# Split weights at a chosen distance modulo 256 bytes, and squares written over dead tiles

## The chip, the cores and the metric

The kernel runs on one core of one Trainium2 chip. The metric is the device time of one execution in microseconds, from runs of the same program; one further execution was profiled, and all rows below come from it.

## What is computed

Two layers over 256 frames of width 2048, each an RMS norm, one wide input projection, two groups of mixers and an output projection that is added to the residual; a last RMS norm ends it. Cut to its frame:

```python
def layer_ab(x, ...):
    h = rms_norm(x, norm_g)
    proj = jnp.einsum('btd,de->bte', h, w_in)
    q, k, v, o_pre, z_a, i_pre, f_pre, z_b, xbc, dt_raw = split_cols(proj, SPLIT_AB)
    y_a = mlstm_branch(...)
    y_b = mamba2_branch(...)
    return x + jnp.einsum('bte,ed->btd', jnp.concatenate([y_a, y_b], -1), w_out)

def layer_cd(x, ...):
    h = rms_norm(x, norm_g)
    proj = jnp.einsum('btd,de->bte', h, w_in)
    q_c, ckv, z_c, iq, ik, iw, qkv, z_d, b_pre, a_pre = split_cols(proj, SPLIT_CD)
    y_c = dsa_branch(...)     # top-k attention; keys and values from ckv through w_uk, w_uv
    y_d = gdn_branch(...)     # gated delta rule; q and k are divided by their norms
    return x + jnp.einsum('bte,ed->btd', jnp.concatenate([y_c, y_d], -1), w_out)

return rms_norm(layer_cd(layer_ab(x)))
```

All of it is in float32, and the weights (390 MB) are read once.

## The kernel before

The projections make up most of the work. Weights come in pieces of 1 MB, `load_w`: a DMA fills `wr` (three buffers), ScalarE casts it to `wh` in the faster matmul type (line 191), and VectorE takes the difference `wl` (line 192). `wh` and `wl` have two buffers each, so a cast waits until TensorE is done with the piece before the last. Activations are split in the same way: `hT` (the normed input, 16 blocks of 128 rows), `cT` (the normed latent of the attention, 4 blocks) and the units `ua`, `ub`, `uc` (mixer outputs, 8 blocks each) hold 256 columns of the high part and 256 of the low part per block. A product takes three matmuls, high by high, high by low, low by high. All of them are issued through the helper at line 75; a transpose goes through line 79.

There are two forms. `proj_tok` yields tokens by features in `pt`: the activation is loaded into the array (128 columns) and 512 columns of the weight move through it. `proj_feat` yields features by tokens in `pf`: 128 columns of the weight are loaded, and 256 columns of the activation move. In the names of the trace the moving operand stands first behind the arrow (`pt<-wh,hT`, `pf<-hT,wh`). While one matmul runs, the operand of the next is loaded (PEld in the profile).

`out_proj` is `proj_tok` on a unit. `hT` feeds both forms in both layers, `cT` both forms in the attention. The mixers are generators on the list `steps`; `tick()` runs a piece of the first one between matmuls of the projections, so TensorE's order is interleaved by hand. The list `bg` holds the triangular solve of the delta rule, a long chain on VectorE; each `load_w` runs a piece of it through `pump()`, and a loop of 12 gate projections (`zk`, each `proj_tok` on `hT`) goes on meanwhile. `load_w`'s cast and difference have high priority in the scheduler, which otherwise orders instructions by what they wait for.

In the built program `hT` starts 192 bytes past a multiple of 256 in each partition, the units 160, `cT` 32, and all buffers of `wh` and `wl` 160. The slices that the matmuls read start at multiples of 512 bytes from there. `ones` is a tile of its own beside `tri`, whose right half is also all ones. `gjunk` is a scratch tile for squares whose sums alone are wanted, in the delta rule's query norms (`ssq`, from the transposes in the PSUM tile `qt`) and its output norms (`sso`); `vg` there holds the values.

Of the kernel before, what the change touches and what calls it, by code (L numbers as in the profile page):

```python
# [8 lines left out]
F32 = mybir.dt.float32  # L9
F32R = mybir.dt.float32r  # L10
I32 = mybir.dt.int32
AF = mybir.ActivationFunctionType
# [15 lines left out]
GONE = -3.4e38  # L28

KG, WR, WS = 4, 3, 2  # L30

STEPS = 1150

# [29 lines left out]
def trunk(ctx, tc, x, rel_bias, ab_norm, ab_w_in, ab_ml_b_i, ab_ml_b_f, ab_ml_norm, ab_ssm_conv_w,  # L63
# [4 lines left out]
    V, A, G = nc.vector, nc.scalar, nc.gpsimd  # L68
# [20 lines left out]
    cp = ctx.enter_context(tc.tile_pool(name="cp", bufs=1))  # L89
    wp = ctx.enter_context(tc.tile_pool(name="wp", bufs=3))  # L90
# [10 lines left out]
    tri = cp.tile([128, 256], F32, name="tri")  # L101
    V.memset(tri, 1.0)
    G.affine_select(tri[:, 0:128], tri[:, 0:128], pattern=[[1, 128]], compare_op=OP.is_ge, fill=0.0, base=0, channel_multiplier=-1)
    ones = cp.tile([128, 128], F32, name="ones")
    V.memset(ones, 1.0)

    def mx(name):
        return ps.tile([128, 512], F32, name=name, tag="mx")
# [67 lines left out]
        while steps:  # L176
            tick()

    def load_w(src, r0, nk, pieces, n):

        pump()
        shaped = lambda w: w.rearrange("p k n -> p (k n)").rearrange("p (k n) -> p k n", n=n)
        wr = shaped(wp.tile([128, KG, 512], F32, name="wr", tag="wr", bufs=WR))
        if sum(m for _, m, _ in pieces) < n:
            G.memset(wr[:, 0:nk, 0:n], 0.0)
        for c0, m, at in pieces:
            nc.sync.dma_start(wr[:, 0:nk, at:at + m], src[r0:r0 + nk * 128, c0:c0 + m].rearrange("(k p) n -> p k n", p=128))
        wh = shaped(wp.tile([128, KG, 512], F32R, name="wh", tag="wh", bufs=WS))
        wl = shaped(wp.tile([128, KG, 512], F32R, name="wl", tag="wl", bufs=WS))
        with tc.high_priority():  # L190
            A.copy(wh[:, 0:nk, 0:n], wr[:, 0:nk, 0:n])  # L191
            V.tensor_tensor(wl[:, 0:nk, 0:n], wr[:, 0:nk, 0:n], wh[:, 0:nk, 0:n].bitcast(F32), op=OP.subtract)  # L192
        return wh, wl

    def proj_tok(src, r0, X, c0, n=512, apart=False):

        pts = [ps.tile([128, 512], F32, name=f"pt{t}", tag="pt") for t in range(2)]
        nk = len(X)

        def part(w, k, t):  # L200
            (wh, wl), (xt, i) = w, X[k]
            hi, lo = xt[:, i, t * 128:t * 128 + 128], xt[:, i, 256 + t * 128:384 + t * 128]
            PE.matmul(pts[t][:, :n], hi, wh[:, k % KG, :n], start=k == 0, stop=False)
            PE.matmul(pts[t][:, :n], hi, wl[:, k % KG, :n], start=False, stop=False)
            PE.matmul(pts[t][:, :n], lo, wh[:, k % KG, :n], start=False, stop=k == nk - 1)

        if apart:

            w = [load_w(src, r0 + g * 128, KG, [(c0, n, 0)], n) for g in range(0, nk, KG)]
            for t in range(2):  # L210
                for k in range(nk):
                    part(w[k // KG], k, t)
                    tick()
            return pts
        for g in range(0, nk, KG):
            w = load_w(src, r0 + g * 128, KG, [(c0, n, 0)], n)
            if g + KG == nk:
                order = [(k, t) for t in range(2) for k in range(KG)]
            else:
                order = [(k, t) for k in range(KG) for t in range(2)]  # L220
            for i, (k, t) in enumerate(order):
                part(w, g + k, t)
                if i % 2:
                    tick()
        return pts

    def proj_feat(src, r0, X, pieces, groups=None):

        n = max(p[2] + p[1] for p in pieces)
        n = (n + 127) // 128 * 128  # L230
        nb = n // 128
        pts = [ps.tile([128, 512], F32, name=f"pf{b}", tag="pt") for b in range((nb + 1) // 2)]
        nk = len(X)
        kg = KG * 512 // n
        for g, m in groups or [(g, min(kg, nk - g)) for g in range(0, nk, kg)]:
            wh, wl = load_w(src, r0 + g * 128, m, pieces, n)
            last = g + m == nk
            order = [(k, b) for b in range(nb) for k in range(m)] if last else [(k, b) for k in range(m) for b in range(nb)]
            for at, (k, b) in enumerate(order):
                xt, i = X[g + k]  # L240
                bs = slice(b * 128, b * 128 + 128)
                pt = pts[b // 2][:, b % 2 * 256:b % 2 * 256 + 256]
                PE.matmul(pt, wh[:, k, bs], xt[:, i, 0:256], start=g + k == 0 and b % 2 == 0, stop=False)
                PE.matmul(pt, wh[:, k, bs], xt[:, i, 256:512], start=False, stop=False)
                PE.matmul(pt, wl[:, k, bs], xt[:, i, 0:256], start=False, stop=last and k == m - 1 and (b % 2 == 1 or b == nb - 1))
                if at % nb == nb - 1:
                    tick()
        return pts
# [145 lines left out]
    with ExitStack() as st:  # L394
        mp = st.enter_context(tc.tile_pool(name="mp", bufs=1))
        np1 = ExitStack()
        X, rb = normed(hT, gab, np1.enter_context(tc.tile_pool(name="np1", bufs=1)))
# [49 lines left out]
        pt = mx("RTp")  # L447
# [27 lines left out]
        for i in range(8):  # L475
            k = 1 << i
# [10 lines left out]
        pt = mx("R2Tp")  # L487
# [112 lines left out]
        with tc.tile_pool(name="lp", bufs=1) as lp:  # L600
# [71 lines left out]
            pt = mx("rbp")  # L672
# [10 lines left out]
            for h in range(4):  # L683
# [7 lines left out]
                v = lp.tile([128, 2, 512], F32, name="v", tag="v", bufs=2)  # L691
# [32 lines left out]
    with ExitStack() as st:  # L724
# [3 lines left out]
        X, rb = normed(hT, gcol[:, G_CD:G_CD + 16], kq)  # L728
# [181 lines left out]
        pt = mx("rkp")  # L910
# [197 lines left out]
        with tc.tile_pool(name="gp", bufs=1) as gp:  # L1108
# [13 lines left out]
            for i in range(4):  # L1122
                pts = proj_feat(cd_w_in, 0, X, [(CQKV + i * 512, 512, 0)])
                qc = gp.tile([128, 4, 256], F32, name="qc", tag="qc", bufs=QB)
                ssq = gp.tile([128, 2, 4], F32, name="ssq", tag="ssq", bufs=2)
                junk = gp.tile([128, 128], F32, name="gjunk", tag="gjunk")
                for b in range(2):
                    conv_gate(pts[b], gconv, i * 4 + b * 2, 64, None, qc[:, b * 2:b * 2 + 2].rearrange("p b t -> p (b t)"))
                rq = gp.tile([128, 8], F32, name="rq", tag="rq", bufs=2)
# [2 lines left out]
                def norms(qc, ssq, rq, rq2):  # L1132
                    yield from lag(LQ)
                    for j in range(4):
                        pt = mx("qt")
                        for t in range(2):
                            transpose(pt[:, t * 128:t * 128 + 128], qc[:, j, t * 128:t * 128 + 128])
                        for t in range(2):
                            A.activation(junk, pt[:, t * 128:t * 128 + 128], AF.Square, scale=0.5, accum_out=ssq[:, t, j:j + 1])
                        yield  # L1140

                    rsqrt(rq, ssq.rearrange("p t j -> p (t j)"), 1.0)
                    V.tensor_scalar(rq, rq, scalar1=0.5 * 128 ** -0.5, scalar2=None, op0=OP.mult)
                    V.tensor_tensor(rq2, rq, rq, op=OP.mult)

                steps.append(norms(qc, ssq, rq, rq2))
                for s in range(2):
# [47 lines left out]
                    o = gp.tile([128, 2, 512], F32, name="og_", tag="og_")  # L1195
                    z = gp.tile([128, 2, 512], F32, name="zg", tag="zg")

                    def delta(s, h0, qc, kT, k0, QD, Wt, vf, o, z, rq, rq2):
# [54 lines left out]
                        sso = gp.tile([128, 8], F32, name="sso", tag="sso", bufs=2)  # L1253
                        for c in range(2):
                            for h in range(4):
                                A.activation(junk, o[:, c, hsl[h]], AF.Square, accum_out=sso[:, c * 4 + h:c * 4 + h + 1])

                        dup = lambda r: r.rearrange("p (c j) -> p c j", c=2)[:, :, s * 2:s * 2 + 2].unsqueeze(3).to_broadcast([128, 2, 2, 2])
                        v4 = lambda r: r.rearrange("p (c j r) -> p c j r", c=2, j=2)
# [87 lines left out]
```

## Time and profile before

| | |
|---|---|
| median of 3 runs | 2158.25 us (2156.83 to 2161.36) |
| profiled execution | 2157.74 us, span 2156.0 us |
| granted clock, mean over the span | 0.992 |
| HBM | 389.87 MB read, 193 GB/s over the span |

The span runs from the first to the last instruction of the profile, and the execution's own time has 1.74 us around it. The granted clock is a share of 2.4 GHz. A matmul's printed duration covers its way through the array; consecutive matmuls overlap, so the time that each takes from the stream is the interval between two starts.

### The profile page before, as it was taken

To read this page: it belongs to the slowest core of one execution; us is meant where nothing else is said; L and a number is where in the kernel's file an instruction comes from. 1 tells how busy PE (TensorE), PEld (TensorE's weight loads), DVE (VectorE), ACT (ScalarE), POOL (GpSimd) and SP (SyncE) were. 2 spreads that over 40 slices of the span, in tenths; PEclk is the share of its full clock that TensorE was granted. 3 is DMA by queue.
4 is the path that set the end of the run, shared out by engine and by line. 5 is a ranking of instruction groups with operands and counts; after the bars stand their busy time and mean duration, and the time that the engine had idled before them with its cause. 6 is when DMAs were issued, how large, how long until landed. Compare 5 with 4: busy or idle time off the path is not lost.

```text
span 2156.0 us, 31526 instructions
## 1 busy us (share of the span) xinstructions
PE 2107.7 (98%) x12878; PEld 1861.2 (86%) x12878; DVE 1467.5 (68%) x2096; ACT 993.7 (46%) x1311; POOL 149.6 (7%) x168
## 2 busy tenths in 40 slices
PE   7999999999999999899999999999999999999997
PEld 6989997888889788898878888899898988989986
DVE  7888764555455456578979998555666666766765
ACT  5455443334433444355643333455444444444543
POOL 4000020000000000300100002000000000000001
PEclk9999999999999999999999999999999999999999
DMA  6565456555555555576886666755565555565543
GB/s 184 190 212 176 157 179 215 195 176 176 176 184 187 176 187 185 139 237 221 296 229 202 224 204 207 265 181 181 176 233 180 190 172 189 188 195 182 171 160 124
DMA packets 242342, 415.16 MB, mean 193 GB/s; under 512 B 45093, under 2 KB 69206, under 8 KB 240342
## 3 DMA queue, kind: packets, MB, share of 16 engines
q1 hardware_dynamic: 237254, 389.84, 55.4%
q0 software_dynamic: 4944, 23.31, 3.3%
q8 instruction: 101, 1.65, 0.3%
q14 instruction: 43, 0.35, 0.0%
HBM read 389.87 MB, written 26.38 MB: 193 GB/s over the span
## 4 chain that ended last, share of the span: by engine, by line
PE 85%; DVE 6%; ACT 3%; issue 1%; DMA 1%; ACTq 0%; SPq 0%
PE pt L75 49%; PE pf L75 27%; DVE wl L192 3%; ACT wh L191 2%; PE turn L79 1%; PE py L75 1%; PE pu L75 1%; PE si L75 1%; ACT Dt L862 1%; PE po L75 0%; PE lgt L75 0%; PE num L75 0%; PE pog L75 0%; DMA Dt<-gd 0%; PE vt L79 0%
## 5 line engine op out<-in xcount | busy, mean ns | idle before, releaser
L192 DVE TENSOR_TENSOR wl<-wr,wh 128x2048 fp32r<-128x2048 f32 (+1 forms) x337 | 777.1, 2306 | 482.6 <-ACT wh L191 479.1
L191 ACT CAST wh<-wr 128x2048 fp32r<-128x2048 f32 (+1 forms) x337 | 639.7, 1899 | 774.3 <-PE pt L75 455.4
L75 PE MATMUL pf<-hT,wh 128*128 128x256 f32 x4192 | 768.7, 285 | 0.3 <-POOL hT L296 0.2
L75 PEld LDWEIGHTS pf<-hT,wh 128*128 128x128 f32 x4192 | 650.2, 190 | 9.6 <-issue 5.7
L75 PE MATMUL pf<-hT,wl 128*128 128x256 f32 x2096 | 591.6, 283 | 14.6 <-DVE wl L192 14.6
L75 PE MATMUL pt<-wh,hT 128*128 128x512 f32 x1856 | 593.9, 398 | 0.0
L75 PEld LDWEIGHTS pt<-wh,hT 128*128 128x128 f32 x1856 | 349.2, 188 | 84.4 <-issue 1.9
L75 PEld LDWEIGHTS pf<-hT,wl 128*128 128x128 f32 x2096 | 398.2, 190 | 16.3 <-DVE wl L192 15.4
L75 PE MATMUL pt<-wl,hT 128*128 128x512 f32 x928 | 368.1, 397 | 1.3 <-DVE wl L192 1.3
L75 PE MATMUL pt<-wh,uc 128*128 128x512 f32 x768 | 250.4, 397 | 0.0
L75 PEld LDWEIGHTS pt<-wl,hT 128*128 128x128 f32 x928 | 174.7, 188 | 44.2 <-DVE wl L192 1.9
L75 PEld LDWEIGHTS pt<-wh,uc 128*128 128x128 f32 x768 | 143.9, 188 | 29.0 <-issue 0.5
L75 PE MATMUL pt<-wl,uc 128*128 128x512 f32 x384 | 151.2, 394 | 0.0
L381 DVE SCALAR_TENSOR_TENSOR cy<-pf,gconv,cy 128x255 f32<-128x255 f32 (+2 forms) x192 | 88.4, 477 | 5.3 <-ACT cy L377 3.1
L75 PEld LDWEIGHTS pt<-wl,uc 128*128 128x128 f32 x384 | 72.4, 188 | 13.6 <-DVE wl L192 0.4
L75 PE MATMUL pt<-wh,ua 128*128 128x512 f32 x256 | 80.0, 392 | 0.0
L75 PE MATMUL pt<-wh,ub 128*128 128x512 f32 x256 | 79.1, 389 | 0.0
L350 DVE TENSOR_TENSOR xr<-pt,xr 128x512 f32<-128x512 f32 x80 | 54.9, 686 | 25.5 <-PE pt L75 25.4
L75 PEld LDWEIGHTS pt<-wh,ub 128*128 128x128 f32 x256 | 48.1, 188 | 10.0
L1174 POOL TENSOR_TENSOR QD<-QD,qm 128x256 f32<-128x256 f32 x32 | 22.5, 739 | 491.7 <-DVE nrv L141 257.7
L75 PEld LDWEIGHTS pt<-wh,ua 128*128 128x128 f32 x256 | 47.9, 188 | 9.6
L296 POOL TENSOR_TENSOR hT<-xg,hT 128x512 fp32r<-128x512 f32 x24 | 40.8, 1711 | 201.7 <-issue 123.3
(457 smaller groups left out, 1868.8 us busy)
## 6 DMA issues: line engine op xcount, KB each, us to landing
wr<-in_cd_w_in_dram SPq DMA_DIRECT2D x140, 1024.0 KB, 5.1
wr<-in_ab_w_in_dram SPq DMA_DIRECT2D x87, 1024.0 KB, 5.2
wr<-in_cd_w_out_dram SPq DMA_DIRECT2D x48, 1024.0 KB, 5.1
wr<-in_ab_w_out_dram SPq DMA_DIRECT2D x32, 1024.0 KB, 5.1
wr<-in_ab_w_in_dram SPq DMA_DIRECT2D x33, 512.0 KB, 4.3
zd<-zk SPq DMA_DIRECT2D x12, 512.0 KB, 6.2
Dt<-gd SPq DMA_DIRECT2D x4, 1024.0 KB, 8.4
Dd<-Dt POOLq DMA_DIRECT2D x4, 1024.0 KB, 6.2
```

The lines of the kernel that those rows point to most:

```text
L75: return held(nc.tensor.matmul(*args, **kw))
L79: return held(nc.tensor.transpose(*args, **kw))
L191: A.copy(wh[:, 0:nk, 0:n], wr[:, 0:nk, 0:n])
L192: V.tensor_tensor(wl[:, 0:nk, 0:n], wr[:, 0:nk, 0:n], wh[:, 0:nk, 0:n].bitcast(F32), op=OP.subtract)
L296: L.tensor_tensor(hT[:, both, 256:512], part, hT[:, both, 0:256].bitcast(F32), op=OP.subtract)
L350: V.tensor_tensor(xc, pts[t], xc, op=OP.add)
L381: V.scalar_tensor_tensor(yi[:, s:256], u[:, 0:256 - s], tap(3 - s), yi[:, s:256], op0=OP.mult, op1=OP.add)
L862: A.activation(dc, dc, AF.Abs, bias=ngc[:, c, i * 8 + h:i * 8 + h + 1])
L1174: G.tensor_tensor(QD[:, h], QD[:, h], qm[:, h // 2 * 256:h // 2 * 256 + 256], op=OP.mult)
```

## The change

`load_w` gets a parameter `shift`. Buffers of `wh` and `wl` become 64 elements (256 bytes) longer, and the weights lie in them from element `shift` on. The table `SHIFT` holds a pair for each activation, by the first letter of its tile's name: `proj_tok` uses the first of the pair, `proj_feat` the second. For `hT` 8 elements are 32 bytes and 24 are 96; for `cT` 128 and 192 bytes; for units 0. With the starts above, weight less activation modulo 256 becomes 0 in every token projection and 64 in every feature projection; before it was 224 (`hT`), 128 (`cT`) and 0 (units). Apart from this, `ones` becomes the right half of `tri`, and the squares that went to `gjunk` overwrite the PSUM tile that they were read from (`qt`), or `vg`.

```diff
+PAD, SHIFT = 64, {"h": (8, 24), "c": (32, 48), "u": (0, 0)}
...
-    ones = cp.tile([128, 128], F32, name="ones")
-    V.memset(ones, 1.0)
+    ones = tri[:, 128:256]
...
-    def load_w(src, r0, nk, pieces, n):
+    def load_w(src, r0, nk, pieces, n, shift):
...
-        shaped = lambda w: w.rearrange("p k n -> p (k n)").rearrange("p (k n) -> p k n", n=n)
-        wr = shaped(wp.tile([128, KG, 512], F32, name="wr", tag="wr", bufs=WR))
+        shaped = lambda w: w.rearrange("p (k n) -> p k n", n=n)
+        wr = shaped(wp.tile([128, KG * 512], F32, name="wr", tag="wr", bufs=WR))
...
-        wh = shaped(wp.tile([128, KG, 512], F32R, name="wh", tag="wh", bufs=WS))
-        wl = shaped(wp.tile([128, KG, 512], F32R, name="wl", tag="wl", bufs=WS))
+        wh = shaped(wp.tile([128, KG * 512 + PAD], F32R, name="wh", tag="wh", bufs=WS)[:, shift:shift + KG * 512])
+        wl = shaped(wp.tile([128, KG * 512 + PAD], F32R, name="wl", tag="wl", bufs=WS)[:, shift:shift + KG * 512])
...
     def proj_tok(src, r0, X, c0, n=512, apart=False):
...
+        shift = SHIFT[X[0][0].name[0]][0]
...
     def proj_feat(src, r0, X, pieces, groups=None):
...
+        shift = SHIFT[X[0][0].name[0]][1]
...
-                junk = gp.tile([128, 128], F32, name="gjunk", tag="gjunk")
...
-                            A.activation(junk, pt[:, t * 128:t * 128 + 128], AF.Square, scale=0.5, accum_out=ssq[:, t, j:j + 1])
+                            half = pt[:, t * 128:t * 128 + 128]
+                            A.activation(half, half, AF.Square, scale=0.5, accum_out=ssq[:, t, j:j + 1])
...
-                                A.activation(junk, o[:, c, hsl[h]], AF.Square, accum_out=sso[:, c * 4 + h:c * 4 + h + 1])
+                                A.activation(v[:, c, hsl[h]], o[:, c, hsl[h]], AF.Square, accum_out=sso[:, c * 4 + h:c * 4 + h + 1])
```

The matmuls of the projections keep their order, except for some at the very start. Where squares lose their scratch tile, the scheduler places them anew among ScalarE's casts. The first place is the query norms of the first of four groups of heads, on ScalarE; `cy` and `qc` are the convolution and its gated result. Before:

```order
547 L377 ACTIVATE cy<-pf_12915,gconv 128x256
548 L1139 ACTIVATE gjunk,ssq<-qt 128x128 x3
549 L191 CAST wh<-wr 128x2048
550 L382 ACTIVATE qc<-cy 128x512
551 L1139 ACTIVATE gjunk,ssq<-qt 128x128 x5
552 L191 CAST wh<-wr 128x2048
```

And of the change (its lines are 3 to 5 further down):

```order
547 L382 ACTIVATE cy<-pf_12913,gconv 128x256
548 L1144 ACTIVATE qt,ssq<-qt 128x128 x4
549 L194 CAST wh<-wr 128x2048
550 L387 ACTIVATE qc<-cy 128x512
551 L1144 ACTIVATE qt,ssq<-qt 128x128 x4
552 L194 CAST wh<-wr 128x2048
```

Four squares instead of three stand ahead of the first cast; the second cast has eight ahead of it as before. The second place is the output norms of the first half group, on ScalarE; `u`, `og_` and `pog` belong to the delta rule's output. Before:

```order
566 L1234 COPY u<-pu 128x512
567 L1240 COPY og__13474<-pog 128x512
568 L1256 ACTIVATE gjunk,sso<-og__13474 128x128 x2
569 L191 CAST wh<-wr 128x2048
570 L1256 ACTIVATE gjunk,sso<-og__13474 128x128 x2
571 L191 CAST wh<-wr 128x2048
```

And of the change:

```order
566 L1239 COPY u<-pu 128x512
567 L1245 COPY og__13471<-pog 128x512
568 L1261 ACTIVATE vg,sso<-og__13471 128x128 x3
569 L194 CAST wh<-wr 128x2048
570 L1261 ACTIVATE vg,sso<-og__13471 128x128
571 L194 CAST wh<-wr 128x2048
```

Here three squares instead of two stand ahead of the first cast, and four ahead of the second, as before. The same move is found at four query norms and at seven of the eight output norms.

## Rows read from the trace of the kernel before

**Rows 1.** The page: busy us, share of the span and instructions by engine.

```profile
PE 2107.7 (98%) x12878; PEld 1861.2 (86%) x12878; DVE 1467.5 (68%) x2096; ACT 993.7 (46%) x1311; POOL 149.6 (7%) x168
```

**Rows 2.** The page: chain that ended last, share of the span by engine.

```profile
PE 85%; DVE 6%; ACT 3%; issue 1%; DMA 1%; ACTq 0%; SPq 0%
```

**Rows 3.** Waits: engine, line, waited for; us in total, times, longest us.

```profile
ACT wh L191 <- PE pt L75: 455.4, 155, 6.4
...
ACT wh L191 <- PE pf L75: 238.7, 88, 11.5
...
PE pf L75 <- DVE wl L192: 14.6, 4, 6.0
```

**Rows 4.** Timeline of TensorE near 352, 389 and 433 us: start, length, instruction.

```profile
352.02 0.40 PE L75 MATMUL pt<-wl,hT 128*128 128x512 f32 x1
...
389.35 0.40 PE L75 MATMUL pt<-wh,hT 128*128 128x512 f32 x1
389.58 0.39 PE L75 MATMUL pt<-wh,ub 128*128 128x512 f32 x1
...
432.88 0.39 PE L75 MATMUL pt<-wh,ub 128*128 128x512 f32 x1
```

**Rows 5.** Matmuls with `wh` from 352.02 to 432.89: count, min/median/max ns.

```profile
L75 PE MATMUL pt<-wh,ub x128: 389/389/393, 389.6 to 432.9; 128*128 128x512 f32 x128
L75 PE MATMUL pt<-wh,hT x108: 392/396/796, 351.4 to 389.3; 128*128 128x512 f32 x108
```

**Rows 6.** Windows: busy us and instructions of PE, PEld, DVE, ACT, POOL; clock; DMA.

```profile
353.00:389.00 36.00, 36.00 (x156) 29.00 (x155) 18.38 (x23) 13.59 (x11) 0.00 (x0) 1.00 0.53 176
390.00:426.00 36.00, 36.00 (x160) 29.81 (x160) 20.56 (x15) 13.66 (x8) 0.00 (x0) 1.00 0.61 203
1120.00:1320.00 200.00, 200.00 (x859) 161.03 (x858) 193.61 (x179) 77.23 (x54) 0.00 (x0) 1.00 0.64 211
```

**Rows 7.** Timeline of TensorE near 667, 676, 1366 and 1372 us.

```profile
666.67 0.40 PE L75 MATMUL pf<-hT,wh 128*128 128x256 f32 x2
...
676.36 0.28 PE L75 MATMUL pf<-hT,wl 128*128 128x256 f32 x1
...
1366.08 0.41 PE L75 MATMUL pf<-cT,wh 128*128 128x256 f32 x2
...
1371.72 0.29 PE L75 MATMUL pf<-cT,wl 128*128 128x256 f32 x1
```

**Rows 8.** Windows of tile `pf` alone: busy us of TensorE, instructions, clock, DMA.

```profile
666.67:676.37 9.70, 9.70 (x84) 1.00 0.69 216
1366.08:1371.73 5.65, 5.65 (x50) 1.00 0.85 281
```

**Rows 9.** Matmuls with `wh`, whole execution; `wl` has half as many in each.

```profile
L75 PE MATMUL pf<-hT,wh 128*128 128x256 f32 x4192 | 768.7, 285 | 0.3 <-POOL hT L296 0.2
...
L75 PE MATMUL pt<-wh,hT x1856: 389/396/796, 104.4 to 1336.5; 128*128 128x512 f32 x186
...
L75 PE MATMUL pt<-wh,uc x768: 387/389/590, 1498.9 to 2144.2; 128*128 128x512 f32 x192
...
L75 PE MATMUL pt<-wh,ua x256: 387/389/481, 761.8 to 853.2; 128*128 128x512 f32 x128
```

**Rows 10.** Groups of TensorE on `cT` and `wh`, feature form (`wl`: half as many).

```profile
L75 PE MATMUL pf<-cT,wh 128*128 128x256 f32 x128 | 24.0, 287 | 0.0
```

**Rows 11.** Tile `gjunk`: count, min/median/max ns (one of eight `og_` pairs).

```profile
L1139 ACT ACTIVATE gjunk<-qt x32: 261/277/278, 1586.2 to 2005.6; 128x128 f32<-128x128 f32 x32
L1139 ACT ACTIVATION_READ_ACCUMULATOR gjunk<-qt x32: 194/195/203, 1586.4 to 2005.8; 128x1 f32 x32
L1256 ACT ACTIVATE gjunk<-og__13989 x8: 301/311/312, 1682.9 to 1701.5; 128x128 f32<-128x128 f32 x8
```

**Rows 12.** Line 103 and tile `rbp`: count, ns, first and last start.

```profile
L103 POOL TENSOR_SCALAR_AFFINE_SELECT tri<-tri x1: 298/298/298, 2.4 to 2.4; 128x128 f32<-128x128 f32 x1
...
L75 PE MATMUL rbp<-dg,ones x8: 272/275/422, 22.5 to 860.6; 128*128 128x128 f32 x8
```

More of the change, by code (lines that the diff above doesn't have):

```diff
@@ L207, in proj_tok @@
         if apart:
-            w = [load_w(src, r0 + g * 128, KG, [(c0, n, 0)], n) for g in range(0, nk, KG)]
+            w = [load_w(src, r0 + g * 128, KG, [(c0, n, 0)], n, shift) for g in range(0, nk, KG)]
             for t in range(2):
@@ L215, in proj_tok @@
         for g in range(0, nk, KG):
-            w = load_w(src, r0 + g * 128, KG, [(c0, n, 0)], n)
+            w = load_w(src, r0 + g * 128, KG, [(c0, n, 0)], n, shift)
             if g + KG == nk:
@@ L233, in proj_feat @@
         nk = len(X)
+        shift = SHIFT[X[0][0].name[0]][1]
         kg = KG * 512 // n
         for g, m in groups or [(g, min(kg, nk - g)) for g in range(0, nk, kg)]:
-            wh, wl = load_w(src, r0 + g * 128, m, pieces, n)
+            wh, wl = load_w(src, r0 + g * 128, m, pieces, n, shift)
             last = g + m == nk
```

## Prediction

> **What bounds the kernel now.** I read the head of the page first. TensorE's matmuls cover 2107.7 of 2156.0 us, VectorE's work 1467.5, ScalarE's 993.7 [rows 1], and in the chain that ended last TensorE holds 85% of the span, most of it in two tiles, `pt` (token projections) and `pf` (feature projections) [rows 2]. Then the waits: TensorE lost 14.6 us to a late `wl` in the feature projections and little elsewhere, while ScalarE's cast to `wh` stood idle 455.4 and 238.7 us until TensorE gave a buffer back [rows 3]. So the split weights are ready before they are wanted; TensorE is the bound, and its pace is the price of every microsecond.
>
> A busy TensorE isn't one at its peak, and the printed duration of a matmul covers its latency, so what counts is the interval from start to start. Two neighbouring stretches give it for the token form (512 moving columns). From the start at 352.02 us to that at 389.35 us lie 160 intervals (108 matmuls of `hT` with `wh`, one of which started earlier, at 351.4, and half as many with `wl`): 37.33 / 160 = 233.3 ns. From 389.58 to 432.88 lie 191 intervals of the same form on `ub` (128 with `wh`, 64 with `wl`): 43.30 / 191 = 226.7 ns [rows 4, 5]. Both run without a break at a granted clock of 1.00, that is 2.4 GHz [rows 6], and nothing about the instruction differs but where its operands lie: `wh` and `wl` start 160 bytes past a multiple of 256, the `u` tiles too, `hT` 192 past. Call distance the weight's start less the activation's, modulo 256: it is 0 for `u`, 224 (32 short) for `hT`, 128 for `cT`, whose tile starts at 32.
>
> For the feature form (256 moving columns of the activation, the weight being loaded) `hT` has 84 matmuls from 666.67 to 676.36, 83 intervals of 116.75 ns; `cT` has 48 from 1366.08 to 1371.72 (50 in the window, two of them `hT`'s still in flight), 47 intervals of 120.0 ns [rows 7, 8]. Again two tiles at two distances, with two paces.
>
> **The change, part by part: token projections.** 1856 matmuls with `wh` and half as many with `wl`, 2784 in all, read `hT` in this form [rows 9]. The shift of 8 floats (32 bytes) puts them at distance 0, that of the `u` tiles. Row for row the price is 233.3 less 226.7, 6.6 ns each. The ends are 0 (the tile, not the distance, made the difference) and 6.6. I take 6.6, since two stretches that touch each other show both values. 12 x 96 = 1152 of the 2784 lie in the loop over 12 gate projections that hides the triangular solve; the other 1632 give 1632 x 6.6 = 10.8 us.
>
> In that loop VectorE is nearly the bound: from 1120 to 1320 us it works 193.61 of 200 us, with 859 `pt` matmuls (the first two still running from before) [rows 6]. At 226.7 ns the same matmuls would want 194.3 us, in which VectorE would have to be busy 99.6%; its subtraction for `wl` waits for a cast now and then, so it can't. The whole gain would be 1152 x 6.6 = 7.6 us, and between 0 and that I take half, 3.8 us. The 96 token matmuls on `cT` also go to distance 0; priced like `hT`'s they give 0.6 us. The 1920 on `u` stay at 0 and cost what they cost.
>
> **Feature projections.** 4192 matmuls with `wh` and 2096 with `wl` go from distance 224 to 64 [rows 9], 128 and 64 on `cT` from 128 to 64 [rows 10]. No row stands at 64. Below it, the best pace the trace gives per column is that of distance 0, 226.7 / 512 x 256 = 113.35 ns; above it is 120.0 ns at 128 [rows 8]. So the 6288 lie between a gain of 3.4 x 6288 = 21.4 us and a loss of 3.25 x 6288 = 20.4 us, and the present 116.75 ns is in the middle. I take half the step down, 115.05 ns. That is a choice. Against it: 32 away from 0 already costs the token form its whole step, so 64 may be no better than 128. For it: 32 away from 0 the feature form stands only halfway up, so its dependence on the distance is another one, and of the eight multiples of 32 the trace shows two, neither of which need be its best. Gain 1.7 x 6288 = 10.7 us, and 192 x 5 = 1.0 us on `cT`.
>
> **A rule that speaks against both terms.** The rows show two paces for one form of matmul at one clock [rows 4, 7]. The Trainium skill, TensorE: Matmul & The Clock Gate, Part 2: What happens when you issue a matmul, says that TensorE has two independent read ports, one for the moving operand and one for the weight load, so that loading the next weights takes no read bandwidth from the running matmul. By that rule the distance between the two can't matter and both terms are 0; by the rows they are 26.9 us together. The trace doesn't contradict the rule outright, since `hT` and `u` are different tiles, but it leaves the 6.6 ns unexplained by it.
>
> **The rest.** ScalarE writes its squares over `qt` in PSUM and over `vg` in place of `gjunk`: 32 and 64 instructions of 277 and 311 ns, with a read of the accumulator of 195 ns behind each [rows 11]. The one reads PSUM, the other SBUF, and 34 ns part them; if the place of the result costs as much either way, 32 x 34 ns = 1.1 us on ScalarE. The order rows show a cast standing behind one more square: four times at the query norms, seven times at the output norms. A square and its read take at most 277 + 195 ns, 0.47 us. Behind that cast queue VectorE's `wl` and then TensorE. What hides it is the idle time ahead of the casts, 694.1 us over 337 of them [rows 3]; without it, 11 delays of 0.47 us would cost 5.2 us. I put 0. The separate `ones` goes, and with it a memset; its readers now stand behind the select that makes `tri`, over by 2.8 us, when the first of them, `rbp`, comes at 22.5 us [rows 12]. The tile that goes and the longer buffers move all others by multiples of 256 bytes, so no distance changes except those to the split weights.
>
> **The sum.** 10.8 + 3.8 + 0.6 + 10.7 + 1.0 = 26.9 us off the profiled execution's own 2157.74 us (span 2156.0 and 1.74 around it): 2130.8, so 2131 us. That execution stands 0.5 us under the median of the runs, 2158.25, within what they scatter. Changes under 0.2% (4.3 us) can't be told from none here.
>
> **Rivals.** *Feature pace unchanged.* At 64 the feature form stays at 116.75 ns. For it: the present value is the middle of the bounds. Token terms 15.2 and `cT` 192 x 3.25 = 0.6 remain: 2142 us. Chance 18%.
>
> *Slower: the feature form goes as at 128.* Place: every feature projection, 6288 matmuls. At 120.0 ns they lose 20.4 us, more than the 15.2 of the token form: 2157.7 + 5.2 = 2163 us. It decides from 116.75 + 15.2 / 6288, that is 119.2 ns, upwards. For it: distance 32 in the token form is as bad as anything there, so 64 may lie on the same high level; against it, 128 is the only feature row that is worse. Chance 17%.
>
> *The shift does nothing.* The 6.6 ns belong to the tiles or to their place above the low 8 address bits, so nothing that this change moves matters. 2157.7 us, no change. Against it: `ua`, `ub` and `uc` are different tiles in several places and their durations sit together at 389 ns, `hT`'s at 396 [rows 5, 9]; one pace for three tiles at one distance is hard to have by chance. Chance 10%. By the rule of the Trainium skill on the two ports (TensorE: Matmul & The Clock Gate, Part 2) this is the case to expect; the rows give it no more than that.
>
> *VectorE takes over in the solve loop.* This is inside the forecast as half a loss; with the whole lost, 2134.6, with none, 2127.
>
> **Numbers.** My forecast, a feature form faster by something between 0.4 and 3.4 ns, has 52%, with a range of its own from 2157.7 - 41.7 = 2116 (113.35 ns, no loss in the solve loop, `cT` at 6.65) to 2139. The remaining 3% are effects I don't see. The range 2115 to 2159 leaves out about half of the slower rival and a little below, 12 to 14 in 100. Faster by over 0.2% means under 2153.9: forecast, unchanged feature pace, a sliver of the rest, 74%. Within 0.2%: the dead shift and the lower half of the slower rival, 17%. Slower: 9%.
>
> **What would show it.** Token stretches on `hT` at 226.7 ns instead of 233.3, median duration 389 instead of 396, `ub`'s unchanged. Feature stretches at another interval than 116.75; at 113 the time falls to 2120, at 119.2 it is where it was. In the solve loop VectorE at 99% with new waits of TensorE for `wl`. The `qt` squares at 277 ns or 34 away. The prediction is wrong if the token interval stays at 233, if the feature interval leaves 113 to 120, or if waits for `wl` grow beyond the 3.8 us allowed for.

## The result, and the profile after

| | before | changed |
|---|---|---|
| median of 4 runs, taken together | 2157.54 us (2155.99 to 2161.36) | 2137.89 us (2134.28 to 2140.94) |
| ratio | | 0.9906, 95% interval 0.9885 to 0.9926 |
| profiled execution | 2157.74 us, span 2156.0 us | 2134.28 us, span 2132.6 us |
| granted clock, mean over the span | 0.992 | 0.993 |

The kernel is 0.94% faster: 19.7 us by the medians. The profiled execution of the changed kernel was the fastest of its four, so the two profiles lie 23.5 us apart.

The page of the changed kernel: busy time by engine, and the shares of the chain that ended last [rows 1, 2]. Lines are 3 to 5 further down than before (78 is the helper of the matmuls, 82 the transposes, 194 the cast to `wh`, 195 the subtraction for `wl`).

```profile
PE 2075.6 (97%) x12878; PEld 1844.2 (86%) x12878; DVE 1466.9 (69%) x2095; ACT 986.7 (46%) x1311; POOL 150.0 (7%) x168
PE 82%; DVE 7%; ACT 4%; DMA 2%; issue 1%; ACTq 0%; SPq 0%
```

TensorE is busy 32.1 us less for the same 12878 matmuls. VectorE, ScalarE and the DMAs hold a little more of the chain, 13% in place of 10%.

The token form near the stretch of [rows 4], in the timeline of TensorE:

```profile
348.58 0.40 PE L78 MATMUL pt<-wl,hT 128*128 128x512 f32 x1
...
384.87 0.40 PE L78 MATMUL pt<-wh,hT 128*128 128x512 f32 x1
385.10 0.39 PE L78 MATMUL pt<-wh,ub 128*128 128x512 f32 x1
...
428.42 0.39 PE L78 MATMUL pt<-wh,ub 128*128 128x512 f32 x1
428.65 0.40 PE L78 MATMUL pf<-hT,wh 128*128 128x256 f32 x2
```

And the windows of those two stretches and of the solve loop (columns as in [rows 6]):

```profile
348.58:384.86 36.28, 36.28 (x161) 30.03 (x160) 18.76 (x25) 14.52 (x12) 0.00 (x0) 1.00 0.52 174
385.10:428.40 43.30, 43.30 (x192) 35.86 (x191) 24.42 (x18) 15.79 (x9) 0.00 (x0) 1.00 0.59 194
1100.00:1300.00 200.00, 200.00 (x885) 165.58 (x883) 196.89 (x182) 80.35 (x56) 0.00 (x0) 1.00 0.66 215
```

From 348.58 to 384.87 lie 160 intervals: 226.8 ns, where they were 233.3. On `ub`, 191 intervals from 385.10 to 428.42 give 226.8 as well. The step between the two tiles is gone. In the solve loop 200 us now hold 885 matmuls, and VectorE is busy 98.4% of them.

The median durations of the token form tell the same (group rows of TensorE: count, min/median/max ns) [rows 9]:

```profile
L78 PE MATMUL pt<-wh,hT x1856: 387/389/798, 104.4 to 1316.5; 128*128 128x512 f32 x186
L78 PE MATMUL pt<-wh,uc x768: 387/389/590, 1477.6 to 2120.7; 128*128 128x512 f32 x192
L78 PE MATMUL pf<-hT,wh x4192: 276/276/562, 14.8 to 2015.2; 128*128 128x256 f32 x200
```

The feature form has no single pace. Windows of `pf` alone (columns as in [rows 8], with PEld, VectorE and ScalarE): the first two are the same 84 matmuls of two neighbouring stages, the third is on `cT`, with two of `hT` still in flight.

```profile
428.65:438.10 9.45, 9.45 (x84) 9.45 (x83) 0.00 (x0) 0.00 (x0) 1.00 0.71 224
521.33:531.11 9.78, 9.78 (x84) 9.78 (x83) 0.00 (x0) 0.00 (x0) 1.00 0.69 216
1346.49:1351.83 5.34, 5.34 (x50) 5.34 (x48) 0.00 (x0) 1.17 (x2) 1.00 0.86 312
```

The last matmuls start 0.01 us before the ends: 83 intervals in 9.44 us are 113.7 ns, in 9.77 us 117.7 ns, and 47 on `cT` in 5.33 us 113.4 ns [rows 7, 8]. Looked at interval by interval, every longer stretch settles after 4 to 8 matmuls at 113.33 ns or stays at 117.78 until something interrupts it. Counted in stretches of more than 22 intervals, 3343 stand in stretches of the first kind and 794 in the second; shorter stretches show both paces too.

All intervals of TensorE from start to start, summed over the execution by what the first matmul is and whether the next is a projection too (us):

| | before | changed | difference |
|---|---|---|---|
| feature form on `hT` | 757.2 | 744.2 | -13.0 |
| the same, next matmul a mixer's | 36.2 | 40.7 | +4.5 |
| token form on `hT` | 648.9 | 632.4 | -16.5 |
| the same, next matmul a mixer's | 11.5 | 14.0 | +2.5 |
| on `cT`, both forms | 46.4 | 45.3 | -1.1 |
| all others | | | 0.0 |

So what the projections gain, 30.6 us, is partly given back at the places where TensorE turns to a mixer. Waits of TensorE in the changed kernel (columns as in [rows 3]):

```profile
PE pf L78 <- DVE wl L195: 15.7, 4, 6.2
...
PE kt L82 <- ACT kjunk L881: 2.3, 1, 2.3
...
PE pt L78 <- DVE wl L195: 2.0, 2, 1.3
...
PE turn L82 <- DVE og__15307 L1271: 0.8, 1, 0.8
```

Rows like the last stand there for six of the eight output norms. How one of them comes about is seen in the timeline of VectorE and TensorE:

```profile
1620.78 0.69 DVE L1257 TENSOR_TENSOR og__13471<-pog,og__13471 128x512 f32<-128x512 f32 x1 [4.09 <-PE pog L78]
1621.63 2.29 DVE L195 TENSOR_TENSOR wl<-wr,wh 128x2048 fp32r<-128x2048 f32 x1 [0.16 <-ACT wh L194]
1623.84 0.16 DVE L1266 TENSOR_TENSOR sso<-sso,rq 128x8 f32<-128x8 f32 x1
...
1625.96 0.39 PE L78 MATMUL pf<-hT,wh 128*128 128x256 f32 x2
1626.66 1.66 DVE L1271 SCALAR_TENSOR_TENSOR og__13471<-og__13471,ysc,zg 128x128 f32<-128x128 f32 x6
1627.16 0.30 PE L82 MATMUL turn<-ident,og__13471 128*128 128x128 f32 x1 [0.81 <-DVE og__13471 L1271]
```

The squares of `sso` are done at 1622.8, but a subtraction of 2.29 us stands ahead of the norm on VectorE, and then 14 small operations follow at 0.2 us each. From the addition to the transpose 6.38 us pass, and 6.38 passed before (1642.92 to 1649.30), while the feature projections that fill the time on TensorE got shorter. The interval ahead of the first transpose was 871 to 889 ns and is 1081 to 1095.

### The profile page after: what moved, and what is told of

Its sections match the earlier page's. It is cut to its first block, busy times and chain, and to the rows that moved or that the text cites. A ratio compares the mean times of both kernels' runs of the same rounds, so it can differ in the third digit from the quotient of the medians.

```text
span 2132.6 us, 31514 instructions
## 1 busy us (share of the span) xinstructions
PE 2075.6 (97%) x12878; PEld 1844.2 (86%) x12878; DVE 1466.9 (69%) x2095; ACT 986.7 (46%) x1311; POOL 150.0 (7%) x168
## 4 chain that ended last, share of the span: by engine, by line
PE 82%; DVE 7%; ACT 4%; DMA 2%; issue 1%; ACTq 0%; SPq 0%
PE pt L78 46%; PE pf L78 27%; DVE wl L195 4%; ACT wh L194 2%; PE py L78 1%; PE turn L82 1%; DMA wr<-in_ab_w_in_dram 1%; DMA wr<-in_cd_w_in_dram 1%; PE pu L78 1%; PE si L78 1%; ACT Dt L867 1%; PE po L78 1%; PE lgt L78 0%; PE num L78 0%; DMA Dt<-gd 0%
## 5 line engine op out<-in xcount | busy, mean ns | idle before, releaser
L78 PE MATMUL pf<-hT,wh 128*128 128x256 f32 x4192 | 754.5, 283 | 0.6 <-POOL hT L301 0.4
L78 PE MATMUL pt<-wh,hT 128*128 128x512 f32 x1856 | 581.7, 392 | 0.0
L78 PE MATMUL pt<-wl,hT 128*128 128x512 f32 x928 | 362.2, 390 | 2.0 <-DVE wl L195 2.0
```

Of the source, the lines that this page charges most:

```text
L78: return held(nc.tensor.matmul(*args, **kw))
```

## The experiments

**The pace against the distance, by itself.** A kernel with one activation tile and one pair of weight tiles; streams of 96 matmuls, first in the token form, then in the feature form, each with the weights started `sh` floats later. It leaves out the whole computation of the reference.

```diff
+    def tok(name, sh, reps=4):
+        wh, wl = [w[:, sh:sh + 2048].rearrange("p (k n) -> p k n", n=512) for w in (WH, WL)]
...
+    for j in range(16):
+        gap()
+        tok("t" + L[j], j * 4)
...
+    for j in range(16):
+        gap()
+        feat("f" + L[j], j * 4)
```

> This kernel leaves out the whole computation: it loads x and runs only long streams of 96 matmuls of the two projection forms, the split weight lying at 16 distances of 16 bytes each from the activation, and further streams at distances 0 and 32 (and 64 for the feature form) with 256 bytes added. Theory of the distance: the token form takes 226.7 ns from start to start at 0 and 233 at 224, the feature form 113.7 at 64, 116.7 at 224 and 119 to 120 at 128, and 256 bytes more change nothing. Theory of the place (which tile, which address above the low 8 bits): all distances give one interval for each form, and 256 bytes more may give another. Theory of noise from other engines: without them all streams run at 226.7 and 113.7 or better.

Means of the last 48 intervals of each stream, in ns:

| distance, bytes | 0 | 16 | 32 | 48 | 64 | 80 | 96 | 112 |
|---|---|---|---|---|---|---|---|---|
| token form | 226.7 | 231.7 | 233.3 | 233.3 | 228.9 | 231.1 | 233.3 | 231.1 |
| feature form | 120.0 | 118.3 | 118.3 | 117.8 | 117.8 | 118.7 | 118.6 | 119.9 |

| distance, bytes | 128 | 144 | 160 | 176 | 192 | 208 | 224 | 240 |
|---|---|---|---|---|---|---|---|---|
| token form | 232.4 | 233.3 | 234.3 | 233.3 | 233.3 | 234.6 | 233.3 | 236.7 |
| feature form | 118.8 | 120.0 | 120.0 | 118.2 | 117.8 | 116.7 | 116.7 | 120.0 |

With 256 bytes more, tokens have 226.7 at 0 and 233.3 at 32, features 120.0 at 0 and 118.3 at 32, all as without; only at 64 does the feature form differ, 113.3 in place of 117.8. Windows of the streams at 32 (token), 0, 64 and 64 + 256 (feature), 95 intervals each (in the feature streams the first one, behind the transposes, takes 0.2 us, so their means over all 95 lie some 0.9 ns above the table):

```profile
80.11:102.29 22.18, 22.18 (x96) 17.81 (x95) 1.00 0.00 1
...
441.33:452.82 11.49, 11.49 (x96) 11.49 (x96) 1.00 0.00 0
...
488.63:499.91 11.28, 11.28 (x96) 11.28 (x96) 1.00 0.01 1
...
654.30:665.19 10.89, 10.89 (x96) 10.89 (x96) 1.00 0.00 0
```

One pair of tiles, one clock, nothing but a few bytes' shift, and the paces of the kernel come out: 226.7 and 233.3 at the same distances, 0 and 224, and 116.7 at 224. The rival that they belong to tiles or places falls. Two expected values of the feature form were missed: 118.8 at 128, where the kernel has 120.0, and 117.8 at 64 instead of 113.7. The two values at 64 are the first sign that something besides the distance decides there.

**One half of the change at a time.** All three are the changed kernel with another table; the third keeps only the longer buffers, the shared `ones` and the squares' new places.

```diff
-PAD, SHIFT = 64, {"h": (8, 24), "c": (32, 48), "u": (0, 0)}
+PAD, SHIFT = 64, {"h": (8, 0), "c": (32, 0), "u": (0, 0)}     # token form only
+PAD, SHIFT = 64, {"h": (0, 24), "c": (0, 48), "u": (0, 0)}    # feature form only
+PAD, SHIFT = 64, {"h": (0, 0), "c": (0, 0), "u": (0, 0)}      # the rest only
```

> The change with only the token projections moved to distance 0; the feature projections stay at 224 (128 on cT). Theory that the two forms gain apart from each other: token interval on hT 226.9 ns, feature interval 116.9 as before, 2784 x 6.3 = 17.5 us less the new waits of 2 to 3 us, so 14 to 16 us faster, about 2142 to 2144 us. Rival, that the whole difference of the change came from the squares and the freed scratch: token projections at 233.3 or a time within 3 us of the change, 2138.

> The change with only the feature projections moved to distance 64; token projections on hT stay at 224 and on cT at 128. Theory that the two forms gain apart from each other: feature interval on hT about 114.6 ns instead of 116.9, 6288 x 2.3 = 14.5 us less new waits of 4 to 5 us, so 9 to 11 us faster, about 2147 us. Rival, that the feature form gains only because faster token projections shift what runs beside it: interval 116.9 and about 2157 us.

> The change with all shifts at 0: longer buffers, ones inside tri, and the squares over dead tiles remain. Theory that these cost nothing: 2157 to 2158 us, within 0.2% of the kernel before, waits of TensorE for the output norms as before (0.6 us each). Rival, that the squares' new places among the casts cause the longer waits ahead of the output transposes: 3 to 5 us slower, these waits at 0.9 us or more.

| | median us | ratio to before, 95% | tokens on `hT`, ns | features on `hT`, ns |
|---|---|---|---|---|
| before, same chip | 2157.59 | | 233.3 | 116.9 |
| token form only | 2144.84 | 0.9940, 0.9928 to 0.9952 | 226.9 | 116.9 |
| feature form only | 2150.84 | 0.9960, 0.9948 to 0.9973 | 233.3 | 114.6 |
| the rest only | 2158.69 | 1.0004, 0.9996 to 1.0013 | 233.3 | 117.0 |

(The paces are means over the intervals without a wait.) The halves give 12.8 and 6.8 us, together about the 19.7 of the whole, and the rest costs nothing that these runs can tell. Each shift moves only its own form. The paces are those expected; the times fall short of what was expected, 14 to 16 us for the tokens and 9 to 11 for the features. The intervals of 1.08 to 1.10 us ahead of the output norms' transposes stand in the feature form's profile, not in the other two (871 to 899 ns), so the rival, that the squares' new places make these waits, falls. With tokens alone the solve loop ran 1062 matmuls without a break, started from 1086.33 to 1326.87: 226.7 ns; with both halves a cast there waited 6.16 us for its DMA, and TensorE 1.3 us for the `wl` behind it.

**The other operand moved.** The kernel before with two gaps around `hT`; the weights stay where they were. `hT` then has distance 0 in both forms.

```diff
+    cp.tile([128, 56], F32, name="gap0")
     hT = cp.tile([128, 16, 512], F32R, name="hT")
+    cp.tile([128, 8], F32, name="gap1")
```

> The weights stay where they are in the kernel before, and hT is moved by 224 bytes, so that all its products have distance 0, in the token form and in the feature form; units and cT as before. Theory, the distance alone decides: tokens on hT 226.7 ns in place of 233.3, features 120.0 in place of 116.75 (the sweep's pace at 0). That is -17 us for the tokens (as measured with the token shift alone, up to 18) and 6288 x 3.25 = +20 us for the features: 2158 to 2162 us. Rival, the weights' own place or the longer buffers did it: both intervals as before, 2157.5 us. The verdict is read from the intervals, since the time is nearly the same by both.

Measured: 2157.66 us, ratio 0.9999 (0.9989 to 1.0008). The windows of the same two stages as above, token form and feature form:

```profile
352.88:389.18 36.30, 36.30 (x161) 30.03 (x160) 0.68 (x1) 1.79 (x3) 1.00 0.53 174
...
432.94:442.90 9.96, 9.96 (x84) 9.96 (x83) 0.00 (x0) 0.00 (x0) 1.00 0.64 212
```

160 intervals in 36.31 us are 226.9 ns, and 83 in 9.95 us 119.9 ns: both as the distance says, with the weights untouched. The sums over the execution are -16.6 us for tokens and +19.0 for features, of which 2.6 and -4.4 come back at the mixers; the time is where it was, a little under the 2158 to 2162 us that I expected. The two forms want different distances, and one table entry each is what it takes.

**What decides between the two paces at 64.** Feature streams at one and the same place, entered from different work; each twice, a and b.

```diff
+        for n in (1, 2, 3, 4):
+            gap(n)
+            feat("g%d%s" % (n, r), 16)
...
+        for name, sh in (("s", 0), ("t", 16), ("u", 80)):
+            tok("tok" + name + r, sh, reps=1)
+            feat("d" + name + r, 16)
+        for name, sh in (("s", 0), ("t", 8), ("u", 80)):
+            feat("fea" + name + r, sh, reps=1)
+            feat("e" + name + r, 16)
```

> This kernel leaves out the whole computation of the reference: it runs streams of feature-form matmuls on fixed tiles. All streams g, d and e read the same operands at distance 64 and differ only in what TensorE does ahead of them (1 to 4 transposes, a token stream at distance 0, 64 or 64 + 256 bytes, a feature stream at 0, 32 or 64 + 256); p is g with the weight 256 bytes further on; each is there twice. Theory, the entry decides which of two paces a stream holds: among g, d and e both 113.3 and 117.8 ns occur, a and b of a pair agree for the most part, and each stream holds its pace to its end. Rival, the place decides (the weight's start modulo 512): g, d and e all hold 117.8 ns, as at 64 in the first sweep, and p all 113.3, as at 64 + 256. Second rival, chance: a and b disagree as often as not. The last eight streams step the distance by 4 bytes from 48 to 76, each entered after 4 transposes: by any of the theories only those near 64 should be able to reach 113.3, the others lie at 117 to 120.

After tokens at 0 and at 64, from the timeline: the last token, the first feature matmul, the last one, and the next stream.

```profile
133.20 0.39 PE L64 MATMUL toksa<-WH,X 128*128 128x512 f32 x1
133.43 0.28 PE L75 MATMUL dsa<-X,WH 128*128 128x256 f32 x1
...
144.62 0.28 PE L77 MATMUL dsa<-X,WL 128*128 128x256 f32 x1
...
150.10 0.39 PE L64 MATMUL tokta<-WH,X 128*128 128x512 f32 x1
150.34 0.28 PE L75 MATMUL dta<-X,WH 128*128 128x256 f32 x1
...
161.12 0.28 PE L77 MATMUL dta<-X,WL 128*128 128x256 f32 x1
```

95 intervals take 11.19 us (117.8 ns) in the first and 10.78 us (113.5, settled at 113.33) in the second, on the same operands at the same addresses. After tokens at 64 or 64 + 256 the fast pace holds, after tokens at 0 and after features at 0, 32 and 64 + 256 the slow one, and a and b agree in every pair. The scheduler put the transposes of g and p at the start of the program, so of these 16 streams the first follows tokens at 0 and the others feature streams directly; all are slow, p with its 256 bytes more too. That ends the rival of the place. Of the last eight, entered after transposes, those at 64 and 76 hold 113.3, and the one at 48 holds 123.3, where the first sweep had 117.8.

The stream at 64 among them (below) stands behind four transposes, as the stream at 64 of the first sweep did, which took 11.28 us for the same 96 matmuls at 117.8 ns. The interval between the last transpose and the first matmul is the same in both to 1 ns.

```profile
468.01:478.89 10.88, 10.88 (x96) 10.88 (x96) 1.00 0.01 2
```

So what runs ahead of a stream matters, but the kind of work directly ahead doesn't settle it.

**All distances in steps of 4 bytes**, each feature stream entered from tokens at 0:

```diff
+    for j in range(64):
+        tok("t%02d" % j, j, reps=2)
+        tok("z%02d" % j, 0, reps=1)
+        feat("f%02d" % j, j)
```

> This kernel leaves out the whole computation of the reference: on fixed tiles it runs, for each distance from 0 to 252 bytes in steps of 4, a token-form stream of 48 matmuls at that distance, one of 24 at distance 0, and a feature-form stream of 96 at that distance, which is thus always entered from tokens at distance 0. Theory, the distance modulo 256 in fine steps sets the pace and 0 and 64 are not chosen badly: no token stream is faster than 226.7 ns (0), no feature stream faster than 113.3; the stream at 64 holds 117.8, as it did after tokens at 0 in the second sweep, and the one at 76 may hold 113.3 or 118. Rival, another distance would have been better: some feature stream other than 64 holds 113.3 after tokens at 0, or a token stream away from 0 holds 226.7 or less. In the changed kernel the stretches on hT at 117.8 have 794 of its measured intervals, so a distance that always holds 113.3 would be worth 794 x 4.45 = 3.5 us there.

No token stream is better than 226.6 to 226.7 ns, which is distance 0 (46 matmuls without a break at the start; the streams at 0 between the others, not yet settled, show 226.6 to 229.2); those at 28, 60 and 108 come near, 227.6 ns, and the worst, at 68, 116, 132 and 196, have 239.6 to 239.9. Of the feature streams, those at 76, 88 and 180 hold 113.3, the one at 64 117.8 as before, the others 115.6 to 123.3. So the rival was right in part: after tokens at 0, other distances than 64 are better. Nor is the pace a matter of the distance alone elsewhere: from the first sweep to this one the token stream at 48 goes from 233.3 to 230.0, at 64 from 228.9 to 233.4 and at 176 from 233.3 to 231.0, the feature stream at 96 from 118.6 to 117.3, at 128 from 118.8 to the kernel's 120.0 and at 240 from 120.0 to 117.3. Those that the change rests on, tokens at 0 and at 224, have 226.7 and 233.2 to 233.3 in both.

**A later transpose, alone, and distance 88.** `LT` is the number of ticks between the output norm and its transposes; the attention's four output transposes use the same number and move with them.

```diff
-LQ, LV, LS, LT = 5, 5, 2, 4
+LQ, LV, LS, LT = 5, 5, 2, 6
```

> The changed kernel with the transposes of the normed outputs two ticks later (LT 6 in place of 4). Theory, TensorE came early at these six transposes because the features ahead of them got faster while VectorE's and ScalarE's chain did not: with two more ticks, about 3 us of other matmuls, the intervals of 1081 to 1095 ns ahead of them shrink to some 250 and the kernel gains 6 x 0.85 = 5 us at the most, to 2133 us; the tick costs nothing elsewhere. Rival, something new stands in the way (the transposes push the units' evacuations and the output projections back): intervals shrink, but new waits of the same size turn up at the output projections, and the time stays near 2138.

One run at 2134.18 us, with the six intervals at 118 ns. Then four kernels on one chip: the changed kernel again, 88 for the features, `LT` 6 once more, and both.

```diff
-PAD, SHIFT = 64, {"h": (8, 24), "c": (32, 48), "u": (0, 0)}
+PAD, SHIFT = 64, {"h": (8, 30), "c": (32, 54), "u": (0, 0)}
```

> The changed kernel once more, as it is, on the same chip as the three versions beside it: 2137.9 us as before, within 3 us, ratio 0.9906 to the kernel before.

> The changed kernel with distance 88 in place of 64 for all feature projections, a distance at which the third sweep's stream held 113.3 ns after tokens at 0, where 64 held 117.8. Theory, the entry chooses between two paces at 64 only: every undisturbed feature stretch on hT now holds 113.3, the 794 intervals at 117.8 are gone, 3.5 us less than the changed kernel beside it (2134.4 if that is at 2137.9). Rival, 88 has two paces as well and other entries than tokens at 0 choose the slow one: stretches at 117 to 120 turn up after entries from units, from transposes or from features, and the time is the same or up to 5 us longer.

> The version with LT 6, timed: its one look had the six long waits for the normed outputs gone (118 ns in place of 1081 to 1095) and three new ones of 1.02 us ahead of the matmuls on W2B, that is 6 x 0.97 - 3 x 0.9 = 3.1 us less than the changed kernel (2134.8 if that is at 2137.9). Rival, other waits of the same run (4.2 and 6.2 us at 336 and 37 us) belong to it too and not to that look alone: no difference.

> Both together. If the two add, 3.5 + 3.1 = 6.6 us less than the changed kernel, 2131.3 if that is at 2137.9, which would be the fastest of all. If the faster features only bring TensorE to the next late chain sooner, it ends where LT 6 alone does.

| | median us, 4 runs | ratio to before, 95% |
|---|---|---|
| changed kernel again | 2136.46 | 0.9907, 0.9891 to 0.9924 |
| 88 | 2135.04 | 0.9906, 0.9891 to 0.9921 |
| `LT` 6 | 2133.24 | 0.9894, 0.9879 to 0.9909 |
| both | 2132.69 | 0.9893, 0.9878 to 0.9908 |

At 88 the stretches after tokens are fast as expected: the first row below is the stage whose like took 9.78 us at 64. But the second, entered from a mixer's small matmuls, holds 116.7, and so do 674 intervals in stretches of more than 22. The mean without waits, 114.5 ns, is that of 64 (114.6). This is the rival: no gain that can be told from scatter. Of the theory, the part on entries from tokens held; that the choice exists at 64 only did not.

```profile
521.61:531.05 9.44, 9.44 (x84) 9.44 (x83) 0.00 (x0) 0.00 (x0) 1.00 0.69 224
...
241.40:251.08 9.68, 9.68 (x84) 9.65 (x83) 0.00 (x0) 0.00 (x0) 1.00 0.16 44
```

With `LT` 6 TensorE finds the norm done (timeline, below), and the next thing that is late is the inverse's `Bn`: three intervals of 1.03 us, of which the last row shows 0.64 as idle:

```profile
1630.85 0.28 PE L78 MATMUL pf<-hT,wl 128*128 128x256 f32 x1
1630.97 0.60 PE L82 MATMUL turn<-ident,og__13471 128*128 128x128 f32 x4
...
1641.13 0.41 DVE L1185 TENSOR_TENSOR Bn<-pb,nr 128x256 f32<-128x256 f32 x1
...
1641.59 0.87 PE L78 MATMUL pw<-W2B,Bn 128*64 128x128 f32 x6 [0.64 <-DVE Bn L1185]
```

3.2 us less than the changed kernel beside it, where 3.1 were expected; the intervals of the two ratios overlap, so the time alone doesn't prove it, though the trace shows the six waits gone. Both together add nothing to that which these runs can tell. `LT` 6, with 64 or with 88, has the lowest medians that I have, 1.06 and 1.07% under the kernel before; four runs of each can't rank them.

## Why the prediction came out as it did

**The bound.** Right: TensorE's pace is the price, and the two paces of [rows 4] come from the distance. The sweep shows it without the kernel, and `hT` moved shows it from the other side.

**Token form, 6.6 ns.** Right: 233.3 to 226.8 in the stretches, 233.27 to 226.95 over all intervals without a wait.

**The half loss in the solve loop.** Wrong. I put VectorE at 99.6% and concluded that "it can't". With tokens alone the window of [rows 6] holds 884 matmuls, and VectorE is busy 98.8% of it, close to what I had put:

```profile
1120.00:1320.00 200.00, 200.00 (x884) 165.60 (x883) 197.65 (x180) 80.51 (x55) 0.00 (x0) 1.00 0.65 218
```

TensorE runs through that window without a break all the same, and in the changed kernel 982 matmuls from 1094.16 to 1316.55 do so too, at 226.7 ns. An engine at 99% is a bound only if the other waits for it, and [rows 3] had shown such waits at four places in the feature projections. With tokens alone the loop gave its 7.0 us (1062 intervals by 6.6 ns); with both halves it gave as much but for one wait of 1.5 us, for a `wl` whose piece landed late.

**Feature form, 115.05 ns.** The mean came out at 114.6, close by, but by luck, for a reason that I hadn't seen: no stretch runs at 115. They run at 113.3, the bound that I took from the token form's best pace, or at 117.8, a little slower than before, and the mean is their mixture. The deciding point of the slower rival, 119.2, lies above both. *Feature pace unchanged* falls; *as at 128* is right for neither, though the slow pace comes near.

**The features on `cT`.** 120.0 to 113.4 in the stretch shown, more than the 5 ns put; over all of them 118.9 to 114.0 in the mean, 0.9 us against 1.0.

**The rest.** Put at 0, measured at 1.0004. The squares on `qt` take 264 ns in place of 277, those on `vg` 296 in place of 311 [rows 11], so overwriting is cheaper on both and the 34 ns were no price. Eleven casts standing behind one more square cost nothing that the runs can tell either.

**The sum.** Here is the step that failed: the forecast was 26.9 us and the medians give 19.7. The prices per matmul were, if anything, too small: without waits the intervals on `hT` gained 17.2 us (2716 by 6.32 ns) and 13.7 us (5859 by 2.33), with `cT` 32 in all. I let all of what I put go through to the end, as if nothing else had to be ready earlier, and allowed for one wait, in the solve loop. 8.5 of the 32 us came back between the two profiles: 1.2 us at the six output norms (204 ns each), 3.9 at three places around the start of the solve loop (intervals ahead of `kt` 0.50 to 2.65 us, ahead of `rkp` 0.83 to 1.10, and 1.71 for a `wl` whose piece landed late, where an interval of 0.23 was), 0.7 at the layer boundary (4.37 to 5.08 us), and small ones. The other 3.6 us are the profiled execution's own distance from the median.

Other profiles tell which of these belong to the change. The intervals ahead of the output norms' transposes follow the feature pace: 773 to 779 ns with `hT` moved (features at 119.8 ns), 871 to 899 at 116.9 to 117.0, 1081 to 1101 at 114.6. The wait for the late `wl` stands in both profiles of the changed kernel and in that of the feature form alone (intervals of 1.05 to 2.33 us), but not before, with the other two parts alone or with `hT` moved (0.23 to 0.40). But with `hT` moved, where TensorE gets there no earlier, the interval ahead of `kt` is 1.24 us, ahead of `rkp` 1.11 and at the layer boundary 4.86, so the rises there are in part scatter. That the loss as a whole is real is seen in the halves: without waits their intervals gain 17.4 and 14.4 us, and 12.8 and 6.8 arrive. The list of waits before could have told me some of the places: the layer boundary is one of the four of the feature projections in [rows 3], and further down stand, in the same columns:

```profile
PE turn L79 <- DVE og__13474 L1266: 0.6, 1, 0.6
PE rkp L79 <- DVE rk L904: 0.4, 1, 0.4
```

The first of these stands there for six of the eight output norms. TensorE was already early at such places, and a faster stream ahead of them makes it earlier still; the prediction passed over them with "little elsewhere". The late `wl` and the `kt` that grew most are not in the list: it doesn't show who had only just been in time.

**The rule on the two ports.** The Trainium skill, TensorE: Matmul & The Clock Gate, Part 2: What happens when you issue a matmul, says that loading the next weights takes no read bandwidth from the running matmul. That the distance then can't matter, as the prediction worked out from it, is refuted by the sweeps: the same two instructions, alternating on the same tiles at a granted clock of 1.00, take 226.7 ns per token matmul at distance 0 and up to 239.9 at others. The measurement decides. That the reads of the two operands get in each other's way is the natural reading, but no run here looks at the reads themselves, and none leaves the weight loads out of the stream.

## What to carry to other kernels

Where a stream of matmuls with a weight load each shows two paces for one shape, compare the start of the moving operand with that of the weights modulo 256 bytes, and try a few distances in a small kernel before choosing; the two forms need not want the same one. When a stage of the bounding engine gets shorter by a few per cent, look for work of other engines that fills it just so: its wait is short or absent before, and becomes the next one. A distance whose pace depends on what runs ahead has to be measured in the kernel itself. A saving per instruction is a ceiling; here some two thirds of it arrived.

## What was not expected of the hardware

**One program, two paces.** Which of the two paces a feature stretch takes is settled in its first matmuls and held to the end. Within the second small kernel both passes agree; two small kernels differ at 64 behind the same four transposes (113.3 and 117.8), and in the large kernel the same stage can differ from run to run. The same 82 matmuls ahead of the wait for `wl`, in windows of `pf`, in the changed kernel's first profile:

```profile
852.03:861.24 9.21, 9.21 (x83) 9.21 (x82) 0.00 (x0) 0.00 (x0) 1.00 0.36 116
```

And in its second:

```profile
854.71:864.27 9.56, 9.56 (x83) 9.56 (x82) 0.00 (x0) 0.00 (x0) 1.00 0.32 110
```

81 intervals between their first and last starts, 9.19 and 9.54 us: 113.5 and 117.8 ns. The second profile has 835 intervals at the slow pace in place of 794, counted as above, in partly other stages. The kernel before scatters by as much as the changed one, 5.4 and 6.7 us, so this needn't be what makes the runs differ. What in the entry decides is open.

**Squares into one scratch tile.** ScalarE's squares of the output norms started 0.43 us apart when all went to `gjunk`, before:

```profile
1643.65 0.31 ACT L1256 ACTIVATE gjunk<-og__13474 128x128 f32<-128x128 f32 x1
1643.87 0.19 ACT L1256 ACTIVATION_READ_ACCUMULATOR gjunk<-og__13474 128x1 f32 x1
1644.08 0.31 ACT L1256 ACTIVATE gjunk<-og__13474 128x128 f32<-128x128 f32 x1
```

And 0.30 us apart when each goes to its own slice of `vg`, in the changed kernel:

```profile
1621.81 0.29 ACT L1261 ACTIVATE vg<-og__13471 128x128 f32<-128x128 f32 x1
1622.01 0.19 ACT L1261 ACTIVATION_READ_ACCUMULATOR vg<-og__13471 128x1 f32 x1
1622.10 0.30 ACT L1261 ACTIVATE vg<-og__13471 128x128 f32<-128x128 f32 x1
```

That the next write to one tile waits for the last explains it, but is only argued. It lies off the path here: the kernel with the rest alone gained nothing by it.
